# A hybrid attention, S5 and MoE network on one core: q goes into its transposes without its norm, and k is projected before q

## The chip, the cores and the metric

The kernel runs as one program on 1 core of one Trainium2 chip. The metric is the device time of the whole program in microseconds (us), the median of three runs. The core has five engines that work side by side, each with its own queue of instructions: PE (TensorE, matrix multiplication and transposes), DVE (VectorE), ACT (ScalarE), POOL (GpSimd) and SP (SyncE, which here issues the large loads).

## The reference, cut to what matters

Two layers work on 256 latent tokens and 256 context tokens, 1024 values wide. Only the first half of layer 0, the attention and convolution mixer, is touched by the change:

```python
q, k, v, a, g = jnp.split(h @ w_in, [512, 1024, 1536, 2048], axis=-1)   # 8 heads of 64
q, k = rmsnorm(heads(q), q_g), rmsnorm(heads(k), k_g)     # per token and head, then a gain per column
s_band = einsum(q, k_band) * 64 ** -0.5 + bias            # latent queries on latent keys, masked
s_ctx  = einsum(q, k_ctx) * 64 ** -0.5                    # on context keys
p = softmax(concatenate([s_band, s_ctx]), axis=-1)
o = p_band @ v_band + p_ctx @ v_ctx
u = a * sigmoid(g); u = depthwise_conv(u, 31 taps); conv = silu(layernorm(u))
y = concatenate([o, conv]) @ w_out
```

Context queries attend to context keys alone. After the mixer come a gated feed-forward, then layer 1: an S5 state-space mixer and a mixture of eight experts, which reads most of the weights.

## The kernel before, in words

All 512 tokens (four blocks of 128, context first) stand on the 128 partitions. Matrix products of the projections are made of three passes: each float32 operand is split into a rounded half (wh, hh) and the rest (wl, hl), and `mm3` (L221) multiplies wh by hh, wl by hh and wh by hl. `split` (L190) makes the two halves of a weight unit: ACT casts (L203), and DVE, or POOL for the units named in `ON_POOL` (L2278), subtracts (L205).

`mix_in` (L577) computes the five projections of w_in one after another, in the order of L586: a (3), g (4), q (0), k (1), v (2). Each takes two weight units (kh = 0, 1) of four k-steps, and each k-step has 12 matmuls of 512 columns, so that a projection is 96 matmuls into four PSUM banks. Between k-steps `pump` (L628) hands out background work: taps of the depthwise convolution. Of the four blocks of channels DVE does three (tap_v, L676, 93 instructions in all), and ACT with POOL the fourth (ptap on ACT at L685, then the addition on POOL at L686). MIXV = (3, 3, 2) and MIXP = (1, 1, 3) say how many of each a k-step of q, k and v gets; the rest of DVE's taps are given out in the attention, four to a step (TAPS).

After the projection of q, and again after that of k, the norm is made: ACT squares each bank into a buffer that has two copies (L655), DVE sums each head (L656), `rsqrt` (L494) makes the inverse root of 32 values per partition by three Newton steps in 13 small DVE instructions, each needing the one before, and four DVE multiplications write the normed rows to qn (L658). `turn_qk` (L597) then has PE transpose them (16 transposes, L601) and ACT writes the result with the gain to qk (L602). The transposes of one projection are put between the k-steps of the next one: `rest()` at L624 runs after the sixth of eight k-steps (for the gate's transposes, `glu`, it is the second k-step of q's projection). The tile qn has one buffer, which the attention's probabilities use later.

`attention` (L727) has twelve jobs: four pairs of heads by three sets of queries ("c" context, 0 and 1 the latent halves). For each, PE multiplies q by k (S), `raised` (L750) adds the bias on DVE (latent jobs, L764), takes the negated row maximum on DVE (L760, L765), and ACT raises (L767) with the maximum as bias and the row sum as accumulator. `divided` scales by the reciprocal (L773, L775), PE transposes the probabilities (PT), and PE multiplies them by v (O). Units of ada weights for later stages are consumed between jobs (L334), two raw buffers at a time, as the other two hold the bias tables. When the taps are used up, the convolution's layernorm and silu follow (`conv_out`).

What sets the order: in the stage "mix" ACT, POOL and SP run in program order (ORDERED, L2315), and PE and DVE in the order that a planner chooses before the run by its own costs, taking what it takes to be ready, earlier program lines first. In "attention" only SP is in program order. On the chip each engine then runs its list in order, and an instruction that has to wait holds up the ones behind it. So a tap that the planner put ahead of a norm's step stays ahead of it.

Of the kernel before, what the change touches and what calls it, by code (L numbers as in the profile page):

```python
# [156 lines left out]
class Kernel:  # L157
# [80 lines left out]
    def plan(self):  # L238
        a, st = self.a, self.st
        self.g1d = self.dram.tile([P, 64 * 256], F32, name="g1d")  # L240
        self.g2d = self.dram.tile([P, 64 * 256], F32, name="g2d")
        self.rowsd = self.dram.tile([4, D], F32, name="rowsd")
        self.partd = self.dram.tile([4, 4 * D], F32, name="partd")
        self.gated = [[self.dram.tile(shape, F32, name="gated") for shape in ([4, 2 * D], [2, D])] for _ in range(2)]
        self.kd = self.dram.tile([16, 64 * 240], F32, name="kd")
        mi = lambda n, kh: st.add(("mi", n, kh), unit(a["mix_w_in"][n], 4 * kh, 4))
        mix = lambda n: [mi(n, kh) for kh in range(2)]
        part = lambda l, v, n, j: st.add(("ada", l, v, n, j), unit(a["ada_w"][l, 2 * v + n], 4 * j, 4))
        ada = lambda l, v: [part(l, v, n, j) for n in range(2) for j in range(2)]
        for n in range(2):  # L250
            for v in range(2):
                for j in range(2):
                    part(0, v, n, j)
            mi(3, n)
        mix(4), mix(0), mix(1), mix(2)
        for qt in range(2):
            st.add(("bias", qt), a["bias"][:, qt])
        ada(0, 2), ada(0, 3), ada(0, 4)
        for kh in (1, 0):
            for n in range(2):  # L260
                st.add(("mo", n, kh), unit(a["mix_w_out"][n], 4 * kh, 4))
        halves = [(l, v, n) for l, v in ((0, 5), (1, 0), (1, 1), (1, 2), (1, 3), (1, 4), (1, 5)) for n in range(2)]

        def half():
            l, v, n = halves.pop(0)
            for j in range(2):
                part(l, v, n, j)
        for u in range(11):
            st.add(("w1", u), a["ffn_w1"][u])
            if u < 9:  # L270
                half()
            st.add(("w3", u), a["ffn_w3"][u])
            if u < 3:
                half()
            if u in FFN_ENDS:
                lo, hi = FFN_ENDS[u]
                for n in range(2):
                    for f in range(lo, hi, 4):
                        st.add(("w2", f, n), unit(a["ffn_w2"][n], f, min(4, hi - f)))
        half(), half()  # L280
        for j in range(2):
            for kh in range(2):
                st.add(("si", j, kh), a["ssm_w_in"][j, kh].rearrange("p r k f -> p r (k f)"))
        for b in range(8):
            st.add(("g1", b), self.g1d[:, b * UNIT:(b + 1) * UNIT])
        k = self.kd
        add_k = lambda b: st.add(("k", b), bass.AP(tensor=k.tensor, offset=k.offset + b * 16 * 240,
                                                   ap=[[16, 8], [64 * 240, 16], [240, 16], [1, 128]]))
        add_g2 = lambda b: st.add(("g2", b), self.g2d[:, b * UNIT:(b + 1) * UNIT])
        def add_so(j, dh, *zs):  # L290
            for z in zs:
                st.add(("so", dh, j, z), a["ssm_w_out"][dh, j, z])
        add_so(0, 0, 0, 1)
        for b in range(2):
            add_k(b)
        for b in range(4):
            add_g2(b)
        for b in (2, 3):
            add_k(b)
        add_g2(4), add_g2(5)  # L300
        add_so(0, 1, 0)
        add_g2(6), add_g2(7)
        add_so(0, 1, 1)
        for dh in range(2):
            add_so(1, dh, 0, 1)
        self.moe_plan()
# [187 lines left out]
    def rsqrt(self, ss, n, count):  # L494

        V = self.nc.vector
        v, y, t = (self.wk([P, n], name, 1) for name in ("nv", "ny", "nt"))
        V.tensor_scalar(v, ss, 1.0 / count, EPS, op0=OP.mult, op1=OP.add)
        V.tensor_scalar(y.bitcast(I32), v.bitcast(I32), 1, None, op0=OP.logical_shift_right)
        V.tensor_scalar(y.bitcast(I32), y.bitcast(I32), -1, 0x5f3759df, op0=OP.mult, op1=OP.add)  # L500
        V.tensor_scalar(v, v, -0.5, None, op0=OP.mult)
        for _ in range(3):
            V.tensor_tensor(t, y, y, op=OP.mult)
            V.tensor_tensor(t, t, v, op=OP.mult)
            V.scalar_tensor_tensor(y, t, 1.5, y, op0=OP.add, op1=OP.mult)
        return y

    def chain(self, xn, xT, perm=False):

# [67 lines left out]
    def mix_in(self, second):  # L577
# [5 lines left out]
        qg = self.const.tile([P, 1], F32, name="qg")  # L583
        nc.vector.tensor_scalar(qg, self.cols[:, C_QG:C_QG + 1], 0.125, None, op0=OP.mult)
        gains = (qg, self.cols[:, C_KG:C_KG + 1])
        order = [(n, kh) for n in (3, 4, 0, 1, 2) for kh in range(2)]  # L586

        def glu():
            for cb in range(4):
# [15 lines left out]
        for i, (n, kh) in enumerate(order):  # L605
# [5 lines left out]
            for k in range(4):  # L611
                bh, bl = self.piece(("mi", n, kh), k, 0, 512)
                kk = kh * 4 + k
                for t in range(4):
                    s = slice(t * P, (t + 1) * P)
                    self.mm3(pb[t], self.hh[:, kk, s], self.hl[:, kk, s], bh, bl, kk == 0, kk == 7)
                    if not i:
                        for _ in range(START.count((k, t))):
                            second.pop(0)()
                        if (k, t) == SPLIT1:  # L620
                            self.split(("mi", 3, 1))
                if first:
                    first.pop(0)()
                if rest and k == 1 and (kh if n else not kh):  # L624
                    rest()
                    rest = None
                if i:
                    self.pump(t=10, v=MIXV[n] if n < 3 else 0, p=MIXP[n] if n < 3 else 0)  # L628
# [8 lines left out]
            if n == 3:  # L637
                for t in range(4):
                    nc.scalar.copy(aT[:, t], pb[t])
            elif n == 4:  # L640
                for t in range(4):
                    g = self.wk([P, 512], "gt", 2)
                    nc.scalar.activation(g, pb[t], AF.Tanh, scale=0.5)
                    nc.vector.scalar_tensor_tensor(aT[:, t], g, 1.0, aT[:, t], op0=OP.add, op1=OP.mult)
                rest = glu
            elif n == 2:
                for t in range(4):
                    nc.scalar.copy(self.v[:, t], pb[t])
            else:
                qn = mp.tile([P, 4, 512], F32, name="qn", tag="big")  # L650
                ss = self.wk([P, 32], "qss", 1)
                heads = lambda y: y.rearrange("p (h d) -> p h d", h=8)
                for t in range(4):
                    sq = self.wk([P, 512], "gt", 2)
                    nc.scalar.activation(sq, pb[t], AF.Square)  # L655
                    nc.vector.tensor_reduce(ss[:, t * 8:t * 8 + 8], heads(sq), axis=AX.X, op=OP.add)  # L656
                rs = self.rsqrt(ss, 32, 64)
                first = [lambda t=t, y=pb[t], q=qn, r=rs[:, t * 8:t * 8 + 8]: nc.vector.tensor_tensor(  # L658
                    heads(q[:, t]), heads(y), r[:, :, None].to_broadcast([P, 8, 64]), op=OP.mult) for t in range(4)]
                rest = lambda n=n, qn=qn: turn_qk(n, qn)  # L660

# [65 lines left out]
    def attention(self):  # L727
# [22 lines left out]
        def raised(pr, kind, ss):  # L750

            ps = [prob[:, 2 * turn[0] + i] for i in range(2)]
            turn[0] ^= 1
            parts = [slice(0, 256), slice(256, 512)] if kind == "c" else [slice(0, 512)]
            nms = []
            for h2, s in enumerate(ss):
                nm = self.wk([P, 4], "nm", 4)
                nms.append(nm)
                if kind == "c":
                    nc.vector.tensor_reduce(nm[:, 0:2], s.rearrange("p (a b) -> p a b", a=2), axis=AX.X, op=OP.max,  # L760
                                            negate=True)
                else:
                    b = self.st.get(("bias", kind))
                    nc.vector.tensor_tensor(s[:, 256:512], s[:, 256:512], b[:, 2 * pr + h2, :], op=OP.add)  # L764
                    nc.vector.tensor_reduce(nm[:, 0:1], s, axis=AX.X, op=OP.max, negate=True)  # L765
                for i, c in enumerate(parts):
                    nc.scalar.activation(ps[h2][:, c], s[:, c], AF.Exp, bias=nm[:, i:i + 1], accum_out=nm[:, 2 + i:3 + i])  # L767
            return ps, nms, parts

        def divided(ps, nms, parts):  # L770
# [1569 lines left out]
```

## Time and profile before

| | |
|---|---|
| median of three runs | 1831.35 us (1829.4 to 1832.6) |
| profiled execution | 1829.19 us, its span 1827.4 us |
| PE, DVE, ACT, POOL busy, share of the span | 92%, 63%, 39%, 26% |
| mean granted clock of PE | 0.961 of full speed |

All times in the profile are microseconds from the start of the span of one profiled execution. A row of a timeline gives start, length, engine, line, operation, output and input, the number of instructions merged, and in brackets the idle time before it with what ended it. q's projection ends at about 102 us, k's at about 143 us, v's at about 183 us, and the attention stage at about 260 us.

### The profile page before, as it was taken

The page shows a single profiled execution, that of the slowest core. Times are in us where ns is not written, and L with a number is a line of the kernel's source. Part 1 is how long each engine was busy: PE and PEld are TensorE (multiplying, and loading weights), DVE is VectorE, ACT ScalarE, POOL GpSimd, SP SyncE. Part 2 cuts the span into 40 slices and gives each one's busy share as a digit, 9 for nine tenths or more (in the row PEclk, how much of TensorE's full clock was granted, in tenths as well). Part 3 has the DMA queues.
Part 4 walks back from the last instruction along what each step waited for, and adds up shares of the span by engine and source line. Part 5 has one row for each costly group of instructions (what it writes and reads, how often), then busy time and mean ns, then how long its engine had stood idle before and what let it go on. Part 6 is the DMA issues. An engine that isn't in the chain of part 4 may idle for free.

```text
span 1827.4 us, 23220 instructions
## 1 busy us (share of the span) xinstructions
PE 1679.9 (92%) x8562; PEld 1113.5 (61%) x8562; DVE 1145.8 (63%) x1614; ACT 720.0 (39%) x1069; POOL 469.2 (26%) x541
## 2 busy tenths in 40 slices
PE   6967899998998999998588999999999999999997
PEld 3856366876776778765467765545455645555452
DVE  4999788677587555569878754455535554454552
ACT  4435573432332332366354544333433433343330
POOL 2347047397596630060432000000000000000000
PEclk9988999999998999999698999999999999999999
DMA  8320743664654643356966899999999999999997
GB/s 329 125 80 24 253 151 135 212 226 143 213 180 138 220 165 115 112 194 136 299 280 254 330 421 419 420 420 418 419 420 420 419 419 421 419 420 419 420 420 290
DMA packets 107433, 517.03 MB, mean 283 GB/s; under 512 B 13792, under 2 KB 41696, under 8 KB 48688
## 3 DMA queue, kind: packets, MB, share of 16 engines
q1 hardware_dynamic: 76672, 490.77, 69.2%
q10 hardware_dynamic: 29968, 22.57, 3.9%
q0 software_dynamic: 672, 2.14, 0.4%
q8 instruction: 69, 1.13, 0.2%
q14 instruction: 52, 0.43, 0.1%
HBM read 496.46 MB, written 18.97 MB: 282 GB/s over the span
## 4 chain that ended last, share of the span: by engine, by line
PE 46%; DMA 7%; DVE 7%; ACT 3%; issue 1%; POOL 0%; DVEq 0%; SPq 0%; ACTq 0%; POOLq 0%
PE m L2029 11%; PE y L2063 6%; PE m L223 4%; PE m L224 4%; PE m L225 4%; DMA raw<-in_moe 3%; PE w L223 2%; PE w L224 2%; PE w L225 2%; DMA more<-in_moe 2%; PE y L224 2%; PE y L223 2%; PE y L225 2%; DVE wl L205 1%; DMA U<-in_moe 1%
## 5 line engine op out<-in xcount | busy, mean ns | idle before, releaser
L205 DVE TENSOR_TENSOR wl<-raw,wh 128x1024 fp32r<-128x1024 f32 x152 | 193.9, 1309 | 69.1 <-ACT wh L203 68.4
L203 ACT CAST wh<-raw 128x1024 fp32r<-128x1024 f32 x174 | 175.2, 1047 | 150.7 <-PE w L225 74.5
L2029 PE MATMUL m<-raw,gate 128*64 128x512 f32 x384 | 165.7, 597 | 0.4 <-DMA raw<-in_moe 0.4
L224 PE MATMUL m<-wl,small 128*128 128x512 f32 x336 | 134.4, 400 | 13.0 <-DVE wl L205 13.0
L223 PE MATMUL w<-hh,wh 128*128 128x512 f32 (+1 forms) x384 | 145.3, 379 | 0.0
L224 PE MATMUL w<-hl,wh 128*128 128x512 f32 (+1 forms) x384 | 144.2, 376 | 1.2 <-POOL hl L568 0.6
L225 PE MATMUL w<-hh,wl 128*128 128x512 f32 (+1 forms) x384 | 142.8, 373 | 0.0
L223 PE MATMUL m<-wh,small 128*128 128x512 f32 x336 | 136.4, 406 | 0.0
L225 PE MATMUL m<-wh,small 128*128 128x512 f32 x336 | 133.2, 396 | 0.0
L1849 POOL TENSOR_SCALAR brow<-order 128x128 fp32r<-128x128 f32 x10 | 7.8, 791 | 485.2 <-PE bk L1884 485.2
L2052 DVE TENSOR_TENSOR small<-gT,small 128x512 fp32r<-128x512 f32 x21 | 14.5, 691 | 128.4 <-ACT small L2051 128.4
L2051 ACT CAST small<-gT 128x512 fp32r<-128x512 f32 x21 | 12.3, 585 | 197.4 <-PE gT L2048 197.4
L205 DVE TENSOR_TENSOR wl<-U,wh 128x1024 fp32r<-128x1024 f32 x51 | 62.8, 1265 | 35.9 <-ACT wh L203 35.5
L2029 PE MATMUL m<-more,gate 128*64 128x512 f32 x184 | 83.6, 597 | 1.2 <-DMA more<-in_moe 1.2
L205 POOL TENSOR_TENSOR wl<-raw,wh 128x1024 fp32r<-128x1024 f32 x22 | 55.4, 2530 | 110.0 <-ACT wh L203 110.0
L223 PEld LDWEIGHTS w<-hh,wh 128*128 128x128 f32 x384 | 72.7, 189 | 17.2 <-issue 4.2
L224 PEld LDWEIGHTS m<-wl,small 128*128 128x128 f32 x336 | 64.3, 191 | 30.2 <-DVE wl L205 17.4
L224 PEld LDWEIGHTS w<-hl,wh 128*128 128x128 f32 x384 | 72.8, 190 | 15.0 <-POOL hl L568 2.8
L224 PE MATMUL w<-wl,gh 128*128 128x512 f32 x176 | 72.0, 409 | 10.4 <-DVE wl L205 10.4
L225 PEld LDWEIGHTS w<-hh,wl 128*128 128x128 f32 x384 | 72.5, 189 | 13.0
L2029 PEld LDWEIGHTS m<-raw,gate 128*64 128x64 f32 x384 | 47.0, 136 | 54.3 <-issue 51.0
L2029 PE MATMUL m<-U,gate 128*64 128x512 f32 x176 | 80.0, 596 | 0.0
(438 smaller groups left out, 4172.3 us busy)
## 6 DMA issues: line engine op xcount, KB each, us to landing
raw<-in_moe SPq DMA_DIRECT2D x104, 1024.0 KB, 17.9
U<-in_moe SPq DMA_DIRECT2D x52, 1024.0 KB, 17.8
room<-in_moe SPq DMA_DIRECT2D x52, 1024.0 KB, 15.3
more<-in_moe SPq DMA_DIRECT2D x50, 1024.0 KB, 18.5
raw<-in_ada_w SPq DMA_DIRECT2D x48, 1024.0 KB, 5.2
raw<-in_ffn_w SPq DMA_DIRECT2D x30, 1024.0 KB, 5.6
xres<-in_moe SPq DMA_DIRECT2D x27, 1024.0 KB, 18.1
h<-in_moe SPq DMA_DIRECT2D x26, 1024.0 KB, 18.5
```

The source lines that it names most:

```text
L203: nc.scalar.copy(wh[:, :m], flat[:, h:h + m])
L205: eng.tensor_tensor(wl[:, :m], flat[:, h:h + m], wh[:, :m].bitcast(F32), op=OP.subtract)
L223: nc.tensor.matmul(o, lhsT=ah, rhs=bh, start=start, stop=False)
L224: nc.tensor.matmul(o, lhsT=ah, rhs=bl, start=False, stop=False)
L225: nc.tensor.matmul(o, lhsT=al, rhs=bh, start=False, stop=stop)
L1849: eng.tensor_scalar(self.perm[:, int(FEW[e]), t], self.iota64 if FEW[e] and not beyond else self.iota, pos, mask, op0=OP.is_equal, op1=OP. ...
L2029: nc.tensor.matmul(o[64 * i:64 * i + 64], lhsT=self.few[:, 4 * j + k], rhs=w[i][:, k], start=not j and not k, stop=j == 1 and k == 3, tile ...
L2051: nc.scalar.copy(gh, v)
L2052: nc.vector.tensor_tensor(gl, v, gh.bitcast(F32), op=OP.subtract)
L2063: nc.tensor.matmul(y[64 * n:64 * n + 64], lhsT=t[:, 2 * j + f], rhs=w[:, f, n * 512:n * 512 + 512], start=not c and not j and not f, stop= ...
```

## The change

q is copied unnormed by ACT into qn and transposed as it is. The inverse norm r of each row and head is kept (qr) and goes into the exponential as ACT's scale; since the scores are now larger by 1/r, the bias table is multiplied by 1/r (qi, which `rsqrt` now also returns, by one more instruction) as it is added, and the negated maximum is multiplied by r. k keeps its norm. k is loaded and projected before q. The transposes are placed by projection: the gate's after the second k-step of k's projection, k's after the last k-step of q's, q's after the fourth k-step of v's.

```diff
@@ plan
-        mix(4), mix(0), mix(1), mix(2)
+        mix(4), mix(1), mix(0), mix(2)
@@ rsqrt
-        return y
+        V.scalar_tensor_tensor(t, v, -2.0, y, op0=OP.mult, op1=OP.mult)
+        return y, t
@@ mix_in
-        order = [(n, kh) for n in (3, 4, 0, 1, 2) for kh in range(2)]
+        order = [(n, kh) for n in (3, 4, 1, 0, 2) for kh in range(2)]
...
-                if rest and k == 1 and (kh if n else not kh):
+                if rest and (kh, k) == {1: (0, 1), 0: (1, 3), 2: (0, 3)}.get(n):
...
                     nc.scalar.activation(sq, pb[t], AF.Square)
                     nc.vector.tensor_reduce(ss[:, t * 8:t * 8 + 8], heads(sq), axis=AX.X, op=OP.add)
-                rs = self.rsqrt(ss, 32, 64)
-                first = [lambda t=t, y=pb[t], q=qn, r=rs[:, t * 8:t * 8 + 8]: nc.vector.tensor_tensor(
+                    if not n:
+                        nc.scalar.copy(qn[:, t], pb[t])
+                rs, ri = self.rsqrt(ss, 32, 64)
+                if not n:
+                    self.qr, self.qi = rs, ri
+                first = None if not n else [lambda t=t, y=pb[t], q=qn, r=rs[:, t * 8:t * 8 + 8]: nc.vector.tensor_tensor(
                     heads(q[:, t]), heads(y), r[:, :, None].to_broadcast([P, 8, 64]), op=OP.mult) for t in range(4)]
@@ attention, raised
+                m = len(parts)
+                at = slice(0, 2) if kind == "c" else slice(2 + kind, 3 + kind)
+                r, ri = (y.rearrange("p (t h) -> p t h", t=4)[:, at, 2 * pr + h2] for y in (self.qr, self.qi))
...
-                    nc.vector.tensor_tensor(s[:, 256:512], s[:, 256:512], b[:, 2 * pr + h2, :], op=OP.add)
+                    nc.vector.scalar_tensor_tensor(s[:, 256:512], b[:, 2 * pr + h2, :], ri, s[:, 256:512], op0=OP.mult,
+                                                   op1=OP.add)
                     nc.vector.tensor_reduce(nm[:, 0:1], s, axis=AX.X, op=OP.max, negate=True)
+                nc.vector.scalar_tensor_tensor(nm[:, 0:m], nm[:, 0:m], 1.0, r, op0=OP.mult, op1=OP.mult)
                 for i, c in enumerate(parts):
-                    nc.scalar.activation(ps[h2][:, c], s[:, c], AF.Exp, bias=nm[:, i:i + 1], accum_out=nm[:, 2 + i:3 + i])
+                    nc.scalar.activation(ps[h2][:, c], s[:, c], AF.Exp, scale=r[:, i:i + 1], bias=nm[:, i:i + 1],
+                                         accum_out=nm[:, 2 + i:3 + i])
```

## Rows read from the trace of the kernel before

**Rows 1.** The page, part 1: busy time and instructions of each engine.
```profile
PE 1679.9 (92%) x8562; PEld 1113.5 (61%) x8562; DVE 1145.8 (63%) x1614; ACT 720.0 (39%) x1069; POOL 469.2 (26%) x541
```

**Rows 2.** The page, part 4: the chain that ended last, by engine.
```profile
PE 46%; DMA 7%; DVE 7%; ACT 3%; issue 1%; POOL 0%; DVEq 0%; SPq 0%; ACTq 0%; POOLq 0%
```

**Rows 3.** Windows of 20 us: length, busy time of each engine, PE's clock, DMA.
```profile
100.00:120.00 20.00, 19.34 (x86) 15.66 (x84) 20.00 (x28) 7.18 (x11) 5.68 (x4) 1.00 0.31 97
120.00:140.00 20.00, 6.79 (x24) 5.06 (x23) 20.00 (x30) 6.27 (x9) 7.95 (x5) 0.58 0.19 61
140.00:160.00 20.00, 20.00 (x89) 16.56 (x88) 17.57 (x24) 9.36 (x14) 16.29 (x9) 0.99 0.17 54
160.00:180.00 20.00, 8.70 (x34) 6.65 (x33) 20.00 (x23) 9.32 (x14) 17.69 (x11) 0.66 0.00 0
180.00:200.00 20.00, 15.82 (x95) 8.20 (x95) 17.46 (x36) 12.66 (x31) 0.00 (x0) 0.91 0.45 159
200.00:220.00 20.00, 18.56 (x138) 8.80 (x135) 18.31 (x41) 13.28 (x32) 0.00 (x0) 1.00 0.92 309
220.00:240.00 20.00, 16.41 (x108) 8.48 (x108) 10.03 (x22) 11.97 (x27) 0.92 (x2) 0.91 0.63 220
```

**Rows 4.** Waits of PE, 60 to 260 us: total, times, longest.
```profile
PE qT L601 <- DVE qn L658: 23.8, 2, 12.8
```

**Rows 5.** Timeline of PE: both sets of transposes, first scores, a late load.
```profile
133.21 4.83 PE L601 MATMUL qT<-ident,qn 128*128 128x128 f32 x16 [12.84 <-DVE qn L658]
...
171.89 4.83 PE L601 MATMUL qT<-ident,qn 128*128 128x128 f32 x16 [10.94 <-DVE qn L658]
...
182.73 1.14 PE L742 MATMUL S<-qk 64*128 64x256 f32 x8
...
222.38 1.94 PE L334 MATMUL ada<-raw,sil 128*32 128x512 f32 x8 [3.07 <-DMA raw<-in_ada_w]
```

**Rows 6.** Groups of DVE, 100 to 185.2 us: count, busy, mean ns.
```profile
L676 DVE SCALAR_TENSOR_TENSOR cv<-upad,cols,cv 128x512 f32<-128x512 f32 x61 | 46.7, 811 | 0.0
...
L658 DVE TENSOR_TENSOR qn<-mi,ny 128x512 f32<-128x512 f32 x8 | 5.0, 680 | 0.0
```

**Rows 7.** Timeline of DVE: a Newton step twice, taps, k's sums, the first maximum.
```profile
119.73 1.29 DVE L503 TENSOR_TENSOR nt<-ny 128x32 f32<-128x32 f32 x1
...
129.71 0.18 DVE L503 TENSOR_TENSOR nt<-ny 128x32 f32<-128x32 f32 x1
...
134.86 8.04 DVE L676 SCALAR_TENSOR_TENSOR cv<-upad,cols,cv 128x512 f32<-128x512 f32 x12
145.33 1.28 DVE L656 TENSOR_REDUCE qss<-gt 128x8 f32<-128x512 f32 x2 [2.43 <-ACT gt L655]
...
185.26 1.28 DVE L760 TENSOR_REDUCE nm<-S 128x2 f32<-128x512 f32 x2
```

**Rows 8.** Timeline of POOL: a weight subtraction and the convolution's additions.
```profile
122.77 2.94 POOL L205 TENSOR_TENSOR wl<-raw,wh 128x1024 fp32r<-128x1024 f32 x1
125.68 1.87 POOL L686 TENSOR_TENSOR cv<-cv,ptap 128x512 f32<-128x512 f32 x1
139.52 7.27 POOL L686 TENSOR_TENSOR cv<-cv,ptap 128x512 f32<-128x512 f32 x3 [11.97 <-ACT ptap L685]
149.95 27.16 POOL L686 TENSOR_TENSOR cv<-cv,ptap 128x512 f32<-128x512 f32 x15 [3.16 <-ACT ptap L685]
```

**Rows 9.** Timeline of ACT: squares of q (first line) and of k, last tap.
```profile
111.31 1.20 ACT L655 ACTIVATE gt<-mi 128x512 f32<-128x512 f32 x2 [8.95 <-DVE qss L656]
...
146.10 1.20 ACT L655 ACTIVATE gt<-mi 128x512 f32<-128x512 f32 x2 [0.33 <-DVE qss L656]
...
177.34 0.71 ACT L685 ACTIVATE ptap<-upad,cols 128x512 f32<-128x512 f32 x1
```

**Rows 10.** Groups of ACT, 100 to 186 us: with a scale by column, and a plain copy.
```profile
L602 ACT ACTIVATE qk<-qT,qg 128x512 f32<-128x512 f32 x4 | 2.7, 687 | 13.7 <-PE qT L601 13.7
...
L648 ACT COPY v<-mi 128x512 f32<-128x512 f32 x4 | 2.3, 587 | 3.0 <-PE mi L225 2.7
```

**Rows 11.** Groups of DVE, 185.2 to 262 us (the attention).
```profile
L676 DVE SCALAR_TENSOR_TENSOR cv<-upad,cols,cv 128x512 f32<-128x512 f32 x24 | 17.4, 742 | 0.0
...
L773 DVE RECIPROCAL nm<-nm 128x1 f32<-128x1 f32 x16 | 2.5, 155 | 0.2 <-ACT prob L767 0.2
```

## The prediction, made before the changed kernel was run

> **What bounds the kernel now.** I began with the page. PE is busy 92% of the span [rows 1], so a microsecond in which PE stands still is the first thing to look for. The chain that ended last covers 46 + 7 + 7 + 3 + 1 = 64% of the span [rows 2], some 1170 of 1827 us counted from the end; it begins after 600 us and says nothing of the mixer, which ends at about 260 us. What the mixer loses has to be read from the mixer itself. The windows show two holes there: PE is busy 6.79 of 20 us from 120 and 8.70 of 20 from 160, at a clock of 0.58 and 0.66 [rows 3]. PE's waits name the cause: 23.8 us in two waits for qn [rows 4], 12.84 ahead of q's transposes and 10.94 ahead of k's [rows 5].
>
> It would be easy to stop here and book 24 us. But in the same windows DVE is busy 20.00, 20.00, 17.57 and 20.00 of 20 us [rows 3]. **PE waits for qn because DVE is full**, and it stays nearly full (17.46 and 18.31) up to 220. The first row maximum of the softmax starts at 185.26 [rows 7], 1.4 us after the scores that start at 182.73 and last 1.14 [rows 5]. So at the point where the mixer hands over to the attention DVE is already the later one. A PE that arrives earlier waits there instead of at qn. The question is therefore what the change does to DVE's list, and only secondly what it does to PE.
>
> Why DVE is full: between 100 and 185.2 it runs 61 taps of 0.81 us, 46.7 us [rows 6], and the two norm chains, in which a step of 32 values takes 1.29 us at 119.73 and 0.18 us at 129.71 [rows 7]. The first has POOL's additions beside it, the second comes after the addition that ends at 127.55 [rows 8].
>
> **The change, part by part.**
>
> PE. A projection's matmul takes 20.00/89 = 0.225 us [rows 3]. Today PE stops at 133.21 - 12.84 = 120.4 with 24 matmuls of the second projection left. With k's transposes behind all eight k-steps these 24 run first, 5.4 us, and the stop begins at 125.8. k is now where q was, and its qn comes when q's came, so up to 7.4 us of the first stop remain. The second stop, 10.94, goes, as q's transposes need only ACT's copies. Taken by itself PE gains up to 5.4 + 10.9 = 16.4 us, if nothing else is late.
>
> DVE up to the first maximum, in four terms. (a) The four multiplications of q go: 4 x 0.68 = -2.7 [rows 6]. (b) The 2.43 us that DVE waited for k's squares [rows 7] go, since PE no longer comes late: -2.4; bounds -2.4 and 0. (c) Each chain is longer by one step of 32 values: 0.18 in the first, whose end is quiet, 1.29 in the second, which lies beside POOL's run from 149.95 [rows 8]: +1.5; bounds 0.4 and 2.6. (d) POOL work moves into the first chain. The program order of ACT had q's transposes block the last three of that projection's taps until 139.52, where they ran beside DVE's taps; with the transposes later, two of them come ahead of the block. And the subtraction of a q weight unit that ON_POOL names is now made one projection later. Three POOL instructions more beside the chain, each holding up one step by 1.29 - 0.18 = 1.1: +3.3; bounds 0 and, if every later step of the chain meets one (five of them), 5.5. The sum is -0.3. The number of taps that the planner puts ahead of the first maximum may change by a few, but a tap moved across that point is done on the other side of it: zero, except in a rival.
>
> On (d) the trace shows both outcomes: a chain step of 1.29 us beside POOL [rows 7], but also 12 taps at 8.04/12 = 0.67 each from 134.86, while POOL's three additions took 7.27/3 = 2.4 each instead of 1.87 [rows 8]. [...] Every chain step waits for its predecessor, which leaves POOL its opening, so I keep +3.3.
>
> ACT. Four copies of 128x512 come in, 0.587 each [rows 10], 2.3 us, between q's squares, ahead of POOL's taps in ACT's order. ACT also gets a second per-row operand in each of 32 exponentials: 0.687 against 0.587 for a copy with and without one [rows 10], 0.1 each, 3.2 us in 75 us of attention. ACT is busy 12 to 13 of 20 there [rows 3], so the cover is its own idle time: zero; without the cover 3.2.
>
> DVE in the attention. 24 small multiplications of the maximum, priced by the reciprocal at 0.155 [rows 11]: 3.7 us. The 20 us from 220, in which DVE is busy only 10.03 [rows 3], hide about a quarter: +2.8; bounds 0 and, with a wait of the same length behind each, 7.4. The bias addition changes its form at the same size, 0; bounds -1 and +2.
>
> Given back. PE and the ada loads are early now: the late load of 3.07 us [rows 5] and the 4.2 us that DVE idles from 180 to 220 (20 - 17.46 + 20 - 18.31, [rows 3]) are open to recovery, but most of it is latency within a job. I take -2; bounds -7 and 0.
>
> The order of the loads changes, their number doesn't, and PE waits for none of them today: 0.
>
> Total: -0.3 + 2.8 - 2.0 = +0.5 us at the end of the attention, and everything behind it moves by as much. The profiled execution took 1829.19 us, so 1829.7; the median of the runs lies 2.2 us above the profiled one: **about 1832 us, no change that can be measured** (this kernel's runs spread by 0.17%, so that less than about 0.2%, 3.7 us, can't be told from nothing). By itself this case covers 1828 to 1835.
>
> **The rivals.**
>
> *Partial gain, 1823.* DVE has to do only the taps that stand earlier in the program: 61 of the mix and four of the first step, while of the 93 all but 23 or 24 ran before 185.26 [rows 11], some 70. If the planner puts five fewer ahead (5 x 0.81 = 4.1), and (d) falls on POOL (3.3), the first softmax comes 7 to 8 us sooner, and the taps left fit into the idle 10 us from 220. For it: that idle time. Against it: nothing in the change makes the planner prefer scores to taps.
>
> *Full gain, 1815.* PE's 16.4 us come through. It needs a DVE that catches up by 15 us; four full windows speak against it.
>
> *Slower, 1838.* The squares of q have two buffers, so ACT's third waits until DVE has summed the first; the copies and POOL's taps stand behind it in ACT's order. If the planner puts those sums behind its filling taps, ACT waits as in the first projection today, 8.95 us, instead of 0.33 as in the second [rows 9]. ACT's last tap, today at 177.34, then comes up to 8.6 us later, about 186; the copies of v (2.3) and the first exponential follow it at 188 and more, some 3 us later than now, and to that come 2.8 to 3.7 us of small multiplications with nothing given back: +6 to +7. It decides from a wait of about 5 us on. [...]
>
> That the change doesn't do what it says is possible in one part, the remaining stop ahead of k's transposes, and this is in the sum.
>
> **How the numbers follow.** No change 0.43, partial gain 0.23, full gain 0.10, slower 0.24. Faster by more than 0.2% is 0.33, slower 0.24. The range leaves out the full gain and the far end of the slower case: 1817 to 1840, with the bounds of (d), of the small multiplications and of what is given back inside it.
>
> **What would show it.** PE's second wait (10.94) gone, the first still there at 6 to 11 us; DVE at 20 of 20 from 100 to 180; a new wait of PE of 10 us or more between v's projection and the first transposes of probabilities, with the clock down there; the first maximum at 182 to 188. Wrong: a first maximum before 178 (a gain), or ACT waiting over 5 us for the sums of q (a loss).

## The result and the profile after

The changed kernel takes 1839.95 us (median of 11 runs, 1836.33 to 1843.18), the kernel before 1829.40 in the same session (11 runs, 1822.22 to 1833.23). The ratio of the two is **1.0056, 95% interval 1.0046 to 1.0066**: some 10 us slower, with an interval clear of no change. The profiled execution took 1843.18 us, the slowest of the 11, so the two profiles stand 14.0 us apart.

Where the time went is read by stages, from four starts in each profile: the gate's transposes (uT, PE), the first row maximum (DVE), the first exponential (ACT), and the first matmul of the mixer's output projection (mo, PE). Profiles start up to 1.6 us apart at uT, so lengths are compared, not times of day.

| us | uT to first maximum | to first exponential | to mo | uT to mo |
|---|---|---|---|---|
| before | 100.44 | 0.71 | 74.53 | 175.68 |
| after | 100.28 | 6.43 | 80.80 | 187.51 |
| difference | -0.16 | +5.72 | +6.27 | +11.83 |

Behind mo nothing changes: the next stage begins 56.29 us after mo in the kernel before, 56.23 in the changed one. So the loss is all in the mixer, and half of it lies in front of the first exponential, half behind it.

Lines after the changed part have moved: L648 is now L649, L655 L656, L656 L657, L658 L663, L676 L681, L686 L691, L760 L768, L765 L774, L767 L777, L773 L784. PE's waits, 60 to 290 us, after (total, times, longest), which answer to [rows 4]:

```profile
PE ada L334 <- ACT v L649: 17.5, 1, 17.5
PE qT L602 <- DVE qn L663: 11.4, 1, 11.4
```

The second wait for qn has gone, as planned; a wait of 17.5 us for ACT's copies of v has come in its place, and the two largest waits are now 28.9 us together, where the two for qn were 23.8. Windows after, in the columns of [rows 3]:

```profile
120.00:140.00 20.00, 8.44 (x36) 6.33 (x34) 20.00 (x27) 5.42 (x7) 14.42 (x8) 0.82 0.30 94
140.00:160.00 20.00, 19.75 (x90) 16.63 (x90) 20.00 (x32) 11.21 (x18) 10.39 (x3) 0.84 0.03 9
160.00:180.00 20.00, 11.53 (x51) 8.25 (x49) 20.00 (x24) 9.45 (x14) 19.15 (x11) 0.93 0.17 53
180.00:200.00 20.00, 7.92 (x27) 2.53 (x28) 14.45 (x29) 10.11 (x25) 12.76 (x5) 0.50 0.26 86
```

DVE (third busy figure) is full up to 180, fuller than before. From 180 it has 5.55 us idle, PE works 7.92 us at a granted clock of 0.50, and POOL is busy 12.76 us in a window where it did nothing before. What it does there is told by three timelines after: DVE, POOL and ACT.

```profile
140.70 10.68 DVE L681 SCALAR_TENSOR_TENSOR cv<-upad,cols,cv 128x512 f32<-128x512 f32 x16
151.29 1.27 DVE L657 TENSOR_REDUCE qss<-gt 128x8 f32<-128x512 f32 x2
...
177.23 9.35 DVE L681 SCALAR_TENSOR_TENSOR cv<-upad,cols,cv 128x512 f32<-128x512 f32 x14
186.51 1.28 DVE L768 TENSOR_REDUCE nm<-S 128x2 f32<-128x512 f32 x2
...
194.21 0.17 DVE L784 RECIPROCAL nm<-nm 128x2 f32<-128x2 f32 x1 [4.16 <-ACT prob L777]
```

```profile
145.35 7.19 POOL L691 TENSOR_TENSOR cv<-cv,ptap 128x512 f32<-128x512 f32 x1 [10.54 <-ACT ptap L690]
156.72 36.35 POOL L691 TENSOR_TENSOR cv<-cv,ptap 128x512 f32<-128x512 f32 x16 [4.18 <-ACT ptap L690]
```

```profile
152.01 0.60 ACT L656 ACTIVATE gt<-mi 128x512 f32<-128x512 f32 x1 [4.86 <-DVE qss L657]
...
187.74 0.72 ACT L690 ACTIVATE ptap<-upad,cols 128x512 f32<-128x512 f32 x1 [9.72 <-POOL cv L691]
...
190.42 0.72 ACT L690 ACTIVATE ptap<-upad,cols 128x512 f32<-128x512 f32 x1 [0.61 <-POOL cv L691]
191.04 2.03 ACT L649 COPY v<-mi 128x512 f32<-128x512 f32 x4
192.94 0.60 ACT L777 ACTIVATE prob<-S,nm,ny 128x256 f32<-128x256 f32 x1
```

Read them together. The planner filled DVE's time in front of q's sums with 16 taps in one stretch (140.70 to 151.3), where the kernel before had 12 in front of k's [rows 7]. ACT's third square waits 4.86 us for those sums, and POOL's run begins at 156.72 instead of 149.95 [rows 8]. Then DVE has 14 taps in a row from 177.23 to 186.5, and ACT waits 9.72 us for one POOL addition. In both stretches the POOL addition doesn't come through: the one at 145.35 lasts 7.19 us and ends 1.2 us after the last of the 16 taps, against 1.87 for the one at 125.68 before [rows 8]. ACT runs in program order, so the copies of v and the first exponential stand behind that tap: 6.43 us behind the first maximum, where 0.71 was.

One thing more changed that the stages don't show. DVE's taps in front of the first maximum, as groups (from 80 us on; count, busy, mean ns), before and after:

```profile
L676 DVE SCALAR_TENSOR_TENSOR cv<-upad,cols,cv 128x512 f32<-128x512 f32 x67 | 54.0, 851 | 0.0
L681 DVE SCALAR_TENSOR_TENSOR cv<-upad,cols,cv 128x512 f32<-128x512 f32 x75 | 60.3, 854 | 0.0
```

With the three taps that begin a block of channels, 78 of the 93 now run ahead of the first maximum, 70 before: eight more, 6.3 us.

### The profile page after: what moved, and what is told of

Same layout as the page of the kernel before. It is cut to its first block, busy times and chain, and to the rows that moved or that the text cites. A ratio compares the mean times of both kernels' runs of the same rounds, so it can differ in the third digit from the quotient of the medians.

```text
span 1841.3 us, 23251 instructions
## 1 busy us (share of the span) xinstructions
PE 1687.2 (92%) x8562; PEld 1115.7 (61%) x8562; DVE 1151.9 (63%) x1636; ACT 724.1 (39%) x1073; POOL 484.1 (26%) x541
## 3 DMA queue, kind: packets, MB, share of 16 engines
q8 instruction: 69, 1.13, 0.3%
## 4 chain that ended last, share of the span: by engine, by line
PE 46%; DMA 11%; DVE 7%; POOL 2%; ACT 1%; issue 1%; SPq 0%; ACTq 0%; DVEq 0%; POOLq 0%
PE m L2040 10%; PE y L2074 5%; PE m L224 4%; PE m L223 4%; PE m L225 4%; DMA raw<-in_moe 3%; PE w L224 3%; PE w L225 3%; PE w L223 3%; DMA more<-in_moe 2%; DMA U<-in_moe 2%; PE y L224 2%; PE y L223 2%; PE y L225 1%; DVE wl L205 1%
## 5 line engine op out<-in xcount | busy, mean ns | idle before, releaser
L224 PE MATMUL w<-wl,gh 128*128 128x512 f32 x176 | 71.8, 408 | 9.3 <-DVE wl L205 9.3
```

Of the source, the lines that this page charges most:

```text
L224: nc.tensor.matmul(o, lhsT=ah, rhs=bl, start=False, stop=False)
```

## The experiments

Each was timed in five rounds against the kernel before, in three sessions (e1 to e4, e5 to e8, e9 to e12), and its ratio is to the kernel before in its own session. The stages come from each one's profile, read as above, as differences from before in us:

| | change of | ratio (95% interval) | to first maximum | to first exponential | to mo | sum |
|---|---|---|---|---|---|---|
| changed kernel | | 1.0056 (1.0046, 1.0066) | -0.16 | +5.72 | +6.27 | +11.83 |
| e1 | before | 1.0032 (1.0020, 1.0045) | +0.19 | +0.73 | +6.08 | +7.00 |
| e2 | after | 1.0027 (1.0016, 1.0039) | -0.13 | +5.73 | -1.51 | +4.09 |
| e3 | before | 1.0029 (1.0018, 1.0041) | +2.78 | +0.01 | +0.56 | +3.35 |
| e4 | after | 1.0049 (1.0033, 1.0066) | +1.40 | +0.72 | +8.27 | +10.39 |
| e5 | after | 1.0067 (1.0054, 1.0080) | +2.03 | +0.73 | +8.18 | +10.94 |
| e6 | after | 1.0068 (1.0052, 1.0084) | -0.20 | +5.73 | +4.45 | +9.98 |
| e7 | before | 1.0040 (1.0026, 1.0053) | +7.97 | 0.00 | -0.11 | +7.86 |
| e8 | after | 1.0105 (1.0090, 1.0120) | +13.07 | +0.73 | +8.07 | +21.87 |
| e9 | e3 | 1.0007 (0.9997, 1.0017) | +0.01 | +0.01 | +0.01 | +0.03 |
| e10 | before | 1.0023 (1.0011, 1.0036) | +0.10 | +0.74 | +1.75 | +2.59 |
| e11 | before | 1.0013 (1.0000, 1.0027) | +0.15 | 0.00 | +2.95 | +3.10 |
| e12 | after | 1.0044 (1.0028, 1.0061) | -2.47 | +6.19 | +4.18 | +7.90 |

0.001 of the ratio is 1.8 us. The stages are one profile each, so a gap of about 1 us in them is not to be leaned on; behind the first exponential a gap of 2 us can go with PE's granted clock, as in e6 below (0.87 on the mean from the first maximum to 240 us, 0.80 in the changed kernel).

**e1, the kernel before with the changed softmax alone** (a tile of ones for r and 1/r):

```diff
+        self.qr = self.qi = mp.tile([P, 32], F32, name="ones")
+        nc.gpsimd.memset(self.qr, 1.0)
```

and `raised` as in the changed kernel.

> The kernel before, with the changed softmax alone: the bias, the maximum and the exponential take their per-row factors from a tile of ones, everything else is untouched. Theory A (the loss is the wait of v's copies and the first exponentials behind POOL's taps in ACT's order) expects little: 24 multiplications of 0.15 us and 32 exponentials longer by 0.1 us, partly covered, +1 to +3 us. Theory B (the new softmax instructions lengthen the attention) expects +5 to +7 us, the attention's first weight matmul after it at 266 instead of 260.

Measured 1.0032, +7.0 us by stages, nearly all of it between the first exponential and mo. The softmax's new instructions alone cost over half of the loss (5.9 us by the ratio), in a kernel whose order and copies are those of before. This is the size that theory B expected.

**e2, the changed kernel with the softmax of before** (q's norm is left out of the output): `raised` as before, all else as changed.

> The changed kernel with the softmax of before: the norm of q is left out of the output. Theory A expects most of the loss to stay, +6 to +9 us against the kernel before, PE still waiting some 17 us for the copies of v. Theory B expects the loss to shrink to about half, +4 or less.

Measured 1.0027, +4.1 us by stages. The first exponential is as late as in the changed kernel (+5.73), and the attention makes up 1.5 us of it. So raw transposes of q, in the new order and with POOL's subtractions as they now fall, bring nothing: this is what the change would be worth if the norm were free in the softmax. The size, 4.9 us by the ratio, lies between the two expectations; e1's 0.0032 and this 0.0027 make 0.0059, where the changed kernel has 0.0056.

**e3, the order alone**: k first, both normed.

```diff
-        mix(4), mix(0), mix(1), mix(2)
+        mix(4), mix(1), mix(0), mix(2)
...
-        order = [(n, kh) for n in (3, 4, 0, 1, 2) for kh in range(2)]
+        order = [(n, kh) for n in (3, 4, 1, 0, 2) for kh in range(2)]
...
-                if rest and k == 1 and (kh if n else not kh):
+                if rest and (kh, k) == {1: (0, 1), 0: (1, 1), 2: (1, 1)}.get(n):
```

> k is projected first, q second, both normed as before, transposes at the places of before (after the sixth k-step). Theory A expects no change within 3 us, both waits of PE for qn still there. Theory C (the order itself costs, by the weight unit whose subtraction POOL makes one projection later) expects +4 us or more.

Measured 1.0029, as theory C expected. Projecting k before q, with nothing else changed in the program, costs about what e2 costs. Its place is another, though: the first maximum comes 2.8 us later and the first exponential follows at once.

**e4, raw q in the old order** (q, k, v; the root of q in buffers of its own):

> The norm of q goes into the softmax, but the order stays q, k, v, with the transposes at the places of before; q's root has its own buffers. PE's wait of 12.8 us ahead of q's transposes goes. If DVE sets the pace, as the prediction has it, PE then waits as much longer ahead of k's transposes (20 us or more instead of 10.9) and the time is that of the kernel before plus the softmax's share, +1 to +7 us. If PE's waits were the bound, it is 8 us or more faster.

Measured 1.0049, by stages +10.4. That is e1's price and 3 us more (the two intervals overlap), so raw q does not pay in the old order either, and the loss is larger than the 1 to 7 us expected. PE waits 17.8 us in one piece ahead of k's transposes, where the two waits of before were 12.84 and 10.94 [rows 5].

**e5, the changed kernel with two more buffers for q's squares**, so that ACT doesn't wait for the first sums:

```diff
-                    sq = self.wk([P, 512], "gt", 2)
+                    sq = self.wk([P, 512], "gt" if n or t < 2 else "ntmp", 2)
```

> The changed kernel with four buffers for q's squares instead of two, so that ACT does not wait for DVE's sums (4.86 us). Theory A expects POOL's sixteen taps to start about 6 us earlier and to end before DVE's stream of taps begins, v's copies and the first exponential some 5 us earlier, and 4 to 6 us of the loss back. If the sums are not the cause, no change against the changed kernel.

Measured 1.0067. Its ACT:

```profile
179.79 2.03 ACT L649 COPY v<-mi 128x512 f32<-128x512 f32 x4
189.82 0.56 ACT L777 ACTIVATE prob<-S,nm,ny 128x256 f32<-128x256 f32 x1 [8.00 <-DVE nm L775]
```

The copies of v come 11 us sooner, and ACT then waits 8.00 us for DVE, whose first maximum moved to 188.38, behind the same 14 taps and with 78 taps ahead of it, as in the changed kernel. POOL's run now starts earlier and lies beside two more steps of q's chain. The late ACT is real, but taking it away gains nothing: it hands the lateness to DVE. My first theory, that ACT's wait for the squares makes the loss, fell here.

**e6, ACT's taps later** (MIXP (1, 1, 1) instead of (1, 1, 3)):

> The changed kernel with one tap of POOL per k-step of v instead of three; the other eight go into the attention. The copies of v then stand behind 8 additions of POOL instead of 16. Theory A expects PE's wait for v's copies to fall from 17.5 us to under 8 and the time to come back to that of the kernel before or below it. Theory B expects no change, or a loss, as POOL's taps then run beside the softmax.

Measured 1.0068. All of POOL's taps still stood ahead of the copies of v in ACT's list, and ACT waits the same 9.72 us for POOL at 187.08. The run moved nothing that it was meant to move, and decides nothing on the two theories.

It shows something else. Up to the first exponential its stages are those of the changed kernel, but behind it they are 1.8 us shorter (+4.45 instead of +6.27). After its long wait PE works at a lower clock for another 13 us in the profile of the changed kernel: 0.50 from 190 to 200 us, 0.56 from 200 to 205, 1.00 from 205 to 215. Two matmuls of S take 2.07 us there at 197.19, and 1.12 at 211.59. PE after:

```profile
191.66 3.64 PE L334 MATMUL ada<-raw,sil 128*32 128x512 f32 x16 [17.50 <-ACT v L649]
...
197.19 2.07 PE L751 MATMUL S<-qk 64*128 64x512 f32 x2
```

From the first maximum to 240 us the mean granted clock is 0.80 after (from 186.5 on) and 0.87 in e6 (from 185.8 on). So some 2 us of the changed kernel's last stage may go with the clock in its one profile; whether its other executions had them is not known.

**e7 and e8, the root by one POOL instruction** instead of 12 on DVE, in the kernel before (e7) and in the changed one (e8):

```diff
-        V.tensor_scalar(y.bitcast(I32), v.bitcast(I32), 1, None, op0=OP.logical_shift_right)
...
-            V.scalar_tensor_tensor(y, t, 1.5, y, op0=OP.add, op1=OP.mult)
+        self.nc.gpsimd.tensor_tensor(y, v, self.mh32, op=OP.pow)
```

> The kernel before, with the inverse root made by one instruction of POOL (a power of -0.5 on 32 values) in place of eleven or twelve chained DVE instructions. If DVE's chain beside POOL's taps is what PE waits for, both waits for qn (12.8 and 10.9) fall under 4 us, DVE has 25 us less to do, and the time falls by 10 us or more. If DVE is not the bound, no change.

> The changed kernel with the same power on POOL. As for the kernel before: a gain of 10 us or more against the kernel before if DVE sets the pace; the changed softmax then costs what it costs by itself, so this one is slower than the kernel before with the power by that much (1 to 7 us).

Measured 1.0040 and 1.0105, where a chain that leaves DVE should have helped; PE still waits 19.5 us for qn in e7. POOL and DVE of e7:

```profile
116.51 6.36 POOL L499 TENSOR_TENSOR ny<-nv,mh 128x32 f32<-128x32 f32 x1 [13.98 <-DVE nv L498]
```

```profile
122.90 0.69 DVE L654 TENSOR_TENSOR qn<-mi,ny 128x512 f32<-128x512 f32 x1 [5.34 <-POOL ny L499]
...
168.79 26.02 DVE L672 SCALAR_TENSOR_TENSOR cv<-upad,cols,cv 128x512 f32<-128x512 f32 x23
194.74 1.28 DVE L756 TENSOR_REDUCE nm<-S 128x2 f32<-128x512 f32 x2
```

The power takes 6.36 us, and DVE stands idle 5.34 of it, twice, because the normed rows are next in its list. Ahead of the first maximum stand 74 taps, only four more than before, but 23 of them in one stretch, at 1.13 us each beside POOL's additions instead of 0.67 [rows 7]. By groups up to the first maximum the two chains fall from 24.1 us to 0.3, the taps grow from 54.0 us (67) to 71.8 (71), and the two waits for the power are 10.7: the time that left DVE came back as longer taps and as waits. e7 and e8 therefore don't tell what DVE's chain costs by itself.

**e9, e3 with the names of two units in ON_POOL exchanged.** The subtractions of POOL that are named for q's units came one projection later with q; here they are k's:

```diff
-    {('mi', 0, 0), ('mi', 4, 1), ('mo', 1, 1), ...
+    {('mi', 1, 0), ('mi', 4, 1), ('mo', 1, 1), ...
-    {('mi', 0, 1), ('mi', 2, 0), ('mi', 3, 0), ...
+    {('mi', 1, 1), ('mi', 2, 0), ('mi', 3, 0), ...
```

> Order only (k first, both normed), with the two subtractions that ON_POOL gave to q's weight units given to k's instead, so that POOL makes them as the first after the gates' units, as in the kernel before. Theory O1 (the +5.3 us of the order come from POOL's subtractions that moved beside DVE's first chain and taps: 1.6 us for a tap there instead of 0.8): the ratio falls to 1.0000 to 1.0012, the taps from 89 us on last 0.8 to 1.3 again. Theory O2 (they come from the order itself: transposes later, more taps ahead of the first maximum, 74 where before had 70): the ratio stays at 1.002 to 1.004 and the first maximum stays at 188 to 190 us.

Measured **1.0007 (0.9997 to 1.0017)**, and by stages +0.03 us: with two names exchanged the order costs nothing that can be told from zero. The intervals of e3 and e9 don't meet. Timelines of POOL and of DVE in e3, and then of both in e9:

```profile
90.21 3.35 POOL L686 TENSOR_TENSOR cv<-cv,ptap 128x512 f32<-128x512 f32 x2 [24.89 <-ACT ptap L685]
93.52 2.86 POOL L205 TENSOR_TENSOR wl<-raw,wh 128x1024 fp32r<-128x1024 f32 x1
96.34 6.83 POOL L686 TENSOR_TENSOR cv<-cv,ptap 128x512 f32<-128x512 f32 x4
116.00 2.61 POOL L205 TENSOR_TENSOR wl<-raw,wh 128x1024 fp32r<-128x1024 f32 x1 [12.82 <-ACT wh L203]
```

```profile
89.30 14.43 DVE L676 SCALAR_TENSOR_TENSOR cv<-upad,cols,cv 128x512 f32<-128x512 f32 x9
...
116.24 2.41 DVE L498 TENSOR_SCALAR nv<-qss 128x32 f32<-128x32 f32 x1
```

```profile
87.46 2.49 POOL L205 TENSOR_TENSOR wl<-raw,wh 128x1024 fp32r<-128x1024 f32 x1 [19.09 <-ACT wh L203]
```

```profile
92.72 6.51 DVE L676 SCALAR_TENSOR_TENSOR cv<-upad,cols,cv 128x512 f32<-128x512 f32 x5
...
116.34 0.18 DVE L498 TENSOR_SCALAR nv<-qss 128x32 f32<-128x32 f32 x1
```

In e9 POOL makes the subtraction at 87.46 after 19 us of idleness, ahead of its additions. In e3 it falls at 93.52 among them, and the next one at 116.00, just ahead of the first step of the norm's chain. That step takes 2.41 us instead of 0.18: it starts 0.24 after the subtraction and ends 0.04 after it. Nine taps take 14.43/9 = 1.60 us each, in e9 five take 6.51/5 = 1.30.

The exchange moved a second thing with it: ahead of the first maximum e3 has 74 taps (71 of them in 60.8 us), e9 has 70 (67 in 54.0), as the kernel before. Four taps at 0.67 are 2.7 us, as much as the 2.8 by which e3's first maximum is late. So e9 shows that the names make the price of the order; whether POOL's instructions beside DVE or the four taps that the planner then puts ahead are the cause, theory O1 or this part of O2, it doesn't separate.

**e10 and e11, the softmax's price in two parts.** e10 has the multiplication of the maximum and the new bias addition on DVE, the exponentials as before; e11 the scale in the exponentials and nothing new on DVE. Against e1:

```diff
e10
-                    nc.scalar.activation(..., AF.Exp, scale=r[:, i:i + 1], bias=nm[:, i:i + 1],
+                    nc.scalar.activation(..., AF.Exp, bias=nm[:, i:i + 1],
e11
-                    nc.vector.scalar_tensor_tensor(s[:, 256:512], b[:, 2 * pr + h2, :], ri, s[:, 256:512], op0=OP.mult,
-                                                   op1=OP.add)
+                    nc.vector.tensor_tensor(s[:, 256:512], s[:, 256:512], b[:, 2 * pr + h2, :], op=OP.add)
-                nc.vector.scalar_tensor_tensor(nm[:, 0:m], nm[:, 0:m], 1.0, r, op0=OP.mult, op1=OP.mult)
```

> Kernel before with the changed row maximum and bias addition on DVE alone (24 multiplications by a tile of ones, bias addition with a per-row factor); the exponentials as before. Together with the scale in the exponentials this cost 1.0032 (+5.9 us). Theory D (DVE's small multiplications, in the chain maximum - multiplication - exponential, are the price: 24 at 0.15 to 0.29 us and a hand-over each): 1.0022 to 1.0035 here. Theory X (the exponentials' second operand, 0.1 us in each of 32, is the price): 1.000 to 1.001 here. If the two add up by length (6.6 us of multiplications to 3.1 us of exponentials): 1.0020 to 1.0024.

> Kernel before with a per-row scale (a tile of ones) in the 32 exponentials alone; no multiplication of the maximum, bias addition as before. Theory D: 1.0000 to 1.0008, since ACT is busy only 12 to 13 of 20 us there. Theory X: 1.002 to 1.003. By length (3.1 of 9.7 us): 1.001.

Measured 1.0023 and 1.0013; together 0.0036 against e1's 0.0032, and by stages 2.59 + 3.10 = 5.69 against 7.00. Both parts cost, and the ratios are nearest to the third expectation, by length; neither theory that puts all on one of them fits both, though e11's interval reaches down to 1.0000. The 1.3 us by which e1 exceeds the two are not to be leaned on, as each of the three is read from one profile. DVE of e10 and ACT of e11, 185 to 265 us, as groups (count, busy, mean ns, idle before):

```profile
L772 DVE SCALAR_TENSOR_TENSOR nm<-nm,ones 128x1 f32<-128x1 f32 x16 | 4.6, 290 | 0.0
...
L772 DVE SCALAR_TENSOR_TENSOR nm<-nm,ones 128x2 f32<-128x2 f32 x8 | 1.2, 153 | 0.0
```

```profile
L772 ACT ACTIVATE prob<-S,nm,ones 128x512 f32<-128x512 f32 x16 | 12.4, 780 | 3.5 <-DVE nm L770 2.6 <-DVE S L769 0.9
L772 ACT ACTIVATE prob<-S,nm,ones 128x256 f32<-128x256 f32 x16 | 8.8, 559 | 7.4 <-DVE nm L765 6.2 <-DMA gated<-adsb 1.2
```

The exponentials gain (780 - 687) x 16 + (559 - 472) x 16 = 2.9 us (687 and 472 are the means of the same two shapes before), and the stage grows by 2.95: in this profile the whole length is on the path, although ACT is idle a third of the time there [rows 3]. For DVE's part that doesn't hold: the multiplications are 5.8 us and the bias additions 0.9 us longer (483 instead of 426 ns, 16 times), and e10 grows by 2.59.

**e12, the changed kernel with the exchange of e9.**

> The changed kernel with the same exchange of the two POOL subtractions. Theory O1: 0.003 less than the changed kernel's 1.0056, so 1.002 to 1.0035, and the first maximum about 3 us earlier than 186.5. Theory O2: 1.005 to 1.006.

Measured 1.0044 (1.0028 to 1.0061) against 1.0056, by stages 7.90 against 11.83. The first maximum is 2.3 us sooner, near the 3 expected, and 74 taps stand ahead of it instead of 78. The ratio fell by 0.0012, not by 0.003, into the gap between the two expectations, and the two intervals overlap, so that of the gain only the stages speak. Of their 3.9 us, 2.1 lie behind the first exponential, where e6 has 1.8 of them without the exchange; that part is not shown to come from the exchange. The first exponential stays 6.90 us behind the maximum: ACT waits 9.06 us for POOL here too.

Put together, by the ratios: the softmax alone costs 0.0032 (e1), all the rest 0.0027 (e2), and the sum fits the changed kernel's 0.0056. The softmax's share is shown by experiment. In the rest, the order alone costs as much (e3, 0.0029) and nothing with the exchange (e9, 0.0007); but in the changed kernel the exchange takes away at most a part (e12, 0.0044), and the first exponential stays late, so the cause of the rest is shown in part only. No version here beats the kernel before.

## Why the prediction was right in its range and wrong in its mechanism

It forecast no change, 1832.0. The 1839.95 measured are 8 us more and lie 0.05 us inside the range's end (1840). That is luck: the kernel before ran 2 us faster in that session than the 1831.35 on which the forecast was built, and 1831.35 x 1.0056 is 1841.6. A change clear of the scatter came where none was forecast, nearest to the rival "slower, 1838", which had 0.24. In the prediction's own terms the softmax was to cost 2.8 us and cost 7.0 (e1); all the rest was to give 2.3 (-0.3 - 2.0) and cost 4.1 (e2).

- *DVE sets the pace and PE's gain does not come through*: right. PE lost its second stop, and DVE stayed at 20 of 20 to 180.
- *PE's first stop stays, up to 7.4 us, 6 to 11 in the signs to look for*: 11.44, 4 us over the working's own figure. "Its qn comes when q's came" did not hold: k's transposes begin at 139.04, q's did at 133.21, and the first step of the chain is held up as in e3.
- *A new wait of PE of 10 us or more between v's projection and the transposes of probabilities, clock down*: right, 17.5 us, the window at 0.50.
- *DVE up to the first maximum, sum -0.3*: -0.16 from uT, right in size, with luck in it. The terms that were worked out came: (a) -2.5, (b) -2.7, and for (c) and (d), +4.8 together, both chains grew by 4.7 (24.1 to 28.8). As (d) has it, three steps of the first chain are held up beside POOL that were not before (L498, and one each of L504 and L505: 2.2, 1.1 and 1.1 us). But the number of taps ahead of the maximum, put at zero, rose by eight, +6.3; and the three first taps of the blocks (4.3 to 1.6 us) and the weight subtractions (10.8 to 8.4, one of them now ahead of uT), which no term names, took 5.1 off.
- *The first maximum is the handover to the attention*: **the step that failed first, and all that e2 loses.** The working followed DVE to the first maximum and took the exponential to come right behind it, as in the kernel before. It now comes 6.43 us behind. This is the mechanism of the rival: the sums of q stand behind 16 filling taps, ACT waits 4.86 us, at the rival's 5; the last tap starts at 190.42, after the 186 that the rival gave, as POOL's addition behind 14 more taps holds it up, which the rival did not have. In e2 the +5.73 here, less 1.51 behind it, are the whole loss. Yet e5, which takes ACT's wait away, lowers the sum by 0.9 us only and the timed ratio not at all, as DVE is then late itself.
- *Exponentials: +3.2 us, hidden by ACT's idle time, zero*: **the second step that failed.** 2.95 us of stage (e11, one profile; the ratio gives 0 to 5 us), the bound "without the cover". The idle share of a window was not cover here, where DVE waits for the exponential and ACT for the next maximum in turn. The exponentials of the kernel before (first two lines) wait 3.4 and 4.8 us, all for DVE; those of e1, where only the softmax is changed, are longer and wait longer, 5.7 and 6.2:

```profile
L767 ACT ACTIVATE prob<-S,nm 128x512 f32<-128x512 f32 x16 | 11.0, 687 | 3.4 <-DVE nm L765 1.8 <-DVE cv L676 1.0 <-DVE nm L773 0.4
L767 ACT ACTIVATE prob<-S,nm 128x256 f32<-128x256 f32 x16 | 7.4, 472 | 4.8 <-DVE nm L760 4.8
L774 ACT ACTIVATE prob<-S,nm,ones 128x512 f32<-128x512 f32 x16 | 12.4, 777 | 5.7 <-DVE nm L772 3.4 <-DVE nm L781 1.4 <-DVE S L769 0.9
L774 ACT ACTIVATE prob<-S,nm,ones 128x256 f32<-128x256 f32 x16 | 8.8, 560 | 6.2 <-DVE nm L772 4.8 <-DVE S L769 1.4
```

- *Multiplications of the maximum, +2.8*: right in size, 2.6 us of stage (e10), 4.2 by the ratio (2.0 to 6.6). The price of one was not: 0.29 us for the 16 of 128x1, not the reciprocal's 0.155, so that 5.8 us came in and more than half of them was hidden.
- *Given back, -2.0*: open. In the profile of the changed kernel nothing is given back: +6.27 behind the first exponential, where e1, which has nothing to give back, has +6.08. In e2 it is 1.5 us, and e6 and e12 stand 1.6 and 1.9 below e1; e6's mean granted clock is 0.87 from the first maximum to 240 us, where the changed kernel's is 0.80.

Open: whether e5's buffers and e12's exchange together would bring the changed kernel down to the softmax's price; whether raw transposes of q are worth DVE's 2.7 us once the exchange is made and the softmax is that of before; what a limit on the taps ahead of the first maximum would bring. None was tried. Why the planner puts 16 taps in front of q's sums was not looked into.

## What to carry to other kernels

ACT's idle share in a window did not hide its longer instructions here, where two engines take turns: 2.9 us of longer exponentials came to 2.95 of stage, 6.7 us of DVE's new work to 2.59. Bound each added operand or instruction in such a chain by its full length, not by zero. When stages are put in another order, look through every list that is keyed by name (which engine makes which unit): two names that stayed with the old first projection cost 4 us with the order alone (1.0029 to 1.0007). And count the filling work that a planner puts ahead of the point you care for, before and after: a sum that comes out right can hide eight taps of it.

## What the runs showed of the hardware that was not expected

- A POOL addition of 128x512 that met an unbroken stretch of DVE taps took 7.19 us instead of 1.87, until 1.2 us after the last tap; one such stretch each held ACT's next tap for 9.72 us after and for 9.06 in e12. It is not always so: at 178.20 before, an addition inside a stretch of 13 taps (from 173.55) took 1.29 us, and in e7 POOL's additions went through a stretch of 23 taps, which took 1.13 us each instead of 0.67. What decides between the two was not found. Where steps of a chain and taps alternate beside POOL's additions (before from 150.81 us on, after from 156.96 on), most steps take 1.24 to 1.31 us instead of 0.18.
- In e11 the second per-row operand lengthened an exponential of 128x512 by 93 ns (780 against 687 before) and one of 128x256 by 87 ns (559 against 472).
- A power of 128x32 on POOL takes 6.36 us (e7), longer than three of its additions of 128x512 (1.87 each).
